# Feed-forward layers of a two-layer decoder in activations-stationary blocks, two of eight pairs of feature tiles by Strassen's seven products

## The chip, the core and the metric

The kernel runs on one core of one Trainium2 chip. The metric is the device time of one execution in microseconds (us). TensorE is called PE, VectorE DVE, ScalarE ACT, GpSimd POOL, SyncE SP.

## The reference

Two layers over 256 tokens of 2048 features, in float32. Each has a mixer (layer 0: mLSTM and Mamba-2 heads between w_in and w_out; layer 1: attention between w_qkv and w_o) and a feed-forward part, with a residual add behind each. The change concerns the feed-forward part, whose hidden width D_FF is 5632:

```
def swiglu(x, w_gate, w_up, w_down):
    return (jax.nn.silu(x @ w_gate) * (x @ w_up)) @ w_down
...
    for layer in range(DEPTH):
        xn = rms_norm(x, norm_mix[layer])
        ...
        x = x + swiglu(rms_norm(x, norm_ffn[layer]), *ffn_params[layer])
    return rms_norm(x, final_norm)
```

## The kernel before

The tokens are two tiles of 128 (`NT` = 2). A feature dimension is cut into k-tiles of 128 rows, an output dimension into strips of 512 columns (`STRIP`). Every float32 operand is split into a high part (a cast to fp32r on ACT) and a low part (the rest, a subtraction on DVE), and a product is hi·hi + hi·lo + lo·hi. Weights come as float32 by DMA on SP's queue into `raw` (two k-tiles of a strip, 512 KB), are cast to `wh` and subtracted to `wl` (`chunk`, L194 to L206, in high priority, so they stand early in the queues of ACT and DVE). There are 4 raw buffers and 3 of `wh` and `wl`. Activations stand transposed (features on partitions) in a `KT`, hi and lo side by side.

There are two ways to multiply. `lin_w` (L208) keeps 128x128 weight tiles stationary and streams the activations: per tile one matmul of 512 columns (`wh` with hi and lo, L219) and one of 256 (`wl` with hi, L221); results come out transposed. `lin_a` (L236) keeps activations stationary and streams the weights: per k-tile and token tile three matmuls of 512 columns (L249 to L251); results have tokens on partitions. The feed-forward part uses `lin_w` for gate and up (11 strips each), so `hT` needs no transposes, and `lin_a` for down (4 strips over 44 k-tiles), within `project_add`, which adds each strip to the residual `xres`, takes sums of squares (`sumsq`, ACT) and transposes the strip on PE for the next stage (`transpose_split`, four transposes into one bank `p_tr`, then casts and splits). `row_norm` (L179) turns the sums of squares into the norm's factor along rows: DVE `ss`, `rs`, POOL power `r`, DVE `dg`, and two matmuls `p_rb` on PE that broadcast it. The final norm's chain at the end is the same without `p_rb`.

Work of that kind is put off by `later` and given out by `tick`, once per pair of k-tiles, so that it stands between matmuls in PE's queue. Each engine runs its queue in order; the order is fixed when the program is built. PSUM has eight banks, six for accumulators (`acc_w`, `acc_a`) and two for everything else.

## Time and profile before

| | us |
|---|---|
| runs, median of 3 (lowest to highest) | 2657.42 (2655.51 to 2658.36) |
| the profiled execution | 2657.61 |
| its span in the trace | 2655.8 |
| PE busy | 2634.2 (99%) |
| DVE busy | 1621.2 (61%) |
| ACT busy | 1335.1 (50%) |

The span is the time from the first to the last instruction of the trace; the execution's own time has 1.8 us around it. Busy time is that of the instructions of an engine, and DVE and ACT work beside PE.

### The profile page before, as it was taken

To read this page: it belongs to the slowest core of one execution; us is meant where nothing else is said; L and a number is where in the kernel's file an instruction comes from. 1 tells how busy PE (TensorE), PEld (TensorE's weight loads), DVE (VectorE), ACT (ScalarE), POOL (GpSimd) and SP (SyncE) were. 2 spreads that over 40 slices of the span, in tenths; PEclk is the share of its full clock that TensorE was granted. 3 is DMA by queue.
4 is the path that set the end of the run, shared out by engine and by line. 5 is a ranking of instruction groups with operands and counts; after the bars stand their busy time and mean duration, and the time that the engine had idled before them with its cause. 6 is when DMAs were issued, how large, how long until landed. Compare 5 with 4: busy or idle time off the path is not lost.

```text
span 2655.8 us, 35559 instructions
## 1 busy us (share of the span) xinstructions
PE 2634.2 (99%) x13765; PEld 2246.7 (85%) x13765; DVE 1621.2 (61%) x2128; ACT 1335.1 (50%) x1906; POOL 45.8 (2%) x97
## 2 busy tenths in 40 slices
...
GB/s 231 168 191 182 184 182 204 167 187 219 189 190 182 185 188 185 188 184 189 190 191 190 190 182 169 177 171 163 185 183 190 190 190 190 190 190 206 193 195 160
DMA packets 254345, 496.86 MB, mean 187 GB/s; under 512 B 15656, under 2 KB 16048, under 8 KB 253792
## 3 DMA queue, kind: packets, MB, share of 16 engines
...
HBM read 492.39 MB, written 2.14 MB: 186 GB/s over the span
## 4 chain that ended last, share of the span: by engine, by line
PE 97%; DVE 1%; DMA 1%; issue 0%; ACT 0%; POOL 0%; SPq 0%; ACTq 0%; POOLq 0%; DVEq 0%
PE acc_w L219 35%; PE acc_w L221 18%; PE acc_a L249 13%; PE acc_a L251 13%; PE acc_a L250 13%; PE p_tr L169 1%; PE p_y L574 1%; DVE wl L205 1%; PE p_num L451 0%; DMA raw<-in_l_w_in 0%; PE p_qk L689 0%; PE p_o L719 0%; DMA xin<-in_x 0%; ACT wh L204 0%; PE p_pt L711 0%
## 5 line engine op out<-in xcount | busy, mean ns | idle before, releaser
L205 DVE TENSOR_TENSOR wl<-raw,wh 128x1024 fp32r<-128x1024 f32 (+1 forms) x913 | 1116.7, 1223 | 928.0 <-ACT wh L204 923.0
L204 ACT CAST wh<-raw 128x1024 fp32r<-128x1024 f32 (+1 forms) x913 | 958.9, 1050 | 1150.2 <-PE acc_w L219 551.0
L219 PE MATMUL acc_w<-x,wh 128*128 128x512 f32 x3328 | 1170.8, 397 | 0.0
L221 PE MATMUL acc_w<-x,wl 128*128 128x256 f32 x3328 | 929.1, 279 | 0.0
L219 PEld LDWEIGHTS acc_w<-x,wh 128*128 128x128 f32 x3328 | 624.8, 188 | 149.8
L221 PEld LDWEIGHTS acc_w<-x,wl 128*128 128x128 f32 x3328 | 626.9, 188 | 0.5
L219 PE MATMUL acc_w<-xa,wh 128*128 128x512 f32 x768 | 275.8, 403 | 1.1 <-DVE xa L118 1.1
L221 PE MATMUL acc_w<-xa,wl 128*128 128x256 f32 x768 | 215.9, 283 | 0.0
L219 PEld LDWEIGHTS acc_w<-xa,wh 128*128 128x128 f32 x768 | 145.0, 189 | 34.0 <-ACT wh L204 1.5
L249 PE MATMUL acc_a<-wh,xa 128*128 128x512 f32 x384 | 151.5, 395 | 0.0
L250 PE MATMUL acc_a<-wl,xa 128*128 128x512 f32 x384 | 150.8, 393 | 0.0
L251 PE MATMUL acc_a<-wh,xa 128*128 128x512 f32 x384 | 150.7, 393 | 0.0
L221 PEld LDWEIGHTS acc_w<-xa,wl 128*128 128x128 f32 x768 | 145.6, 190 | 1.0
L249 PE MATMUL acc_a<-wh,ha 128*128 128x512 f32 x352 | 137.5, 391 | 0.0
L251 PE MATMUL acc_a<-wh,ha 128*128 128x512 f32 x352 | 137.0, 389 | 0.0
L250 PE MATMUL acc_a<-wl,ha 128*128 128x512 f32 x352 | 137.0, 389 | 0.0
L249 PE MATMUL acc_a<-wh,hb 128*128 128x512 f32 x352 | 136.9, 389 | 0.0
L251 PE MATMUL acc_a<-wh,hb 128*128 128x512 f32 x352 | 136.9, 389 | 0.0
L250 PE MATMUL acc_a<-wl,hb 128*128 128x512 f32 x352 | 136.9, 389 | 0.0
L249 PE MATMUL acc_a<-wh,mx 128*128 128x512 f32 x256 | 100.4, 392 | 0.0
L251 PE MATMUL acc_a<-wh,mx 128*128 128x512 f32 x256 | 99.7, 390 | 0.0
L250 PE MATMUL acc_a<-wl,mx 128*128 128x512 f32 x256 | 99.6, 389 | 0.0
...
## 6 DMA issues: line engine op xcount, KB each, us to landing
raw<-in_l_w_in SPq DMA_DIRECT2D x191, 512.0 KB, 3.5
raw<-in_l_ffn_gate SPq DMA_DIRECT2D x176, 512.0 KB, 3.5
raw<-in_l_ffn_up SPq DMA_DIRECT2D x176, 512.0 KB, 3.5
raw<-in_l_ffn_down SPq DMA_DIRECT2D x176, 512.0 KB, 4.4
raw<-in_l_w_qkv SPq DMA_DIRECT2D x96, 512.0 KB, 3.6
raw<-in_l_w_out SPq DMA_DIRECT2D x64, 512.0 KB, 4.6
raw<-in_l_w_o SPq DMA_DIRECT2D x32, 512.0 KB, 3.5
rows<-scr POOLq DMA_DIRECT2D x10, 512.0 KB, 6.0
```

Of the source, the lines that this page charges most:

```text
L169: nc.tensor.transpose(pt[:, j * T + t * P:j * T + (t + 1) * P], src[t][:, c:c + P], ident)
L204: nc.scalar.copy(wh[:, ks, :], raw[:, ks, :])
L205: nc.vector.tensor_sub(wl[:, ks, :], raw[:, ks, :], wh[:, ks, :].bitcast(F32))
L219: nc.tensor.matmul(banks[f], wh[:, kk, fs], kt.both(k), start=k == 0, stop=False, skip_group_check=True)
L221: nc.tensor.matmul(banks[f][:, :T], wl[:, kk, fs], kt.parts(k)[0], start=False, stop=k == nk - 1, skip_group_check=True)
L249: nc.tensor.matmul(banks[t], xh[:, ts], wh[:, kk, :], start=k == 0, stop=False)
L250: nc.tensor.matmul(banks[t], xh[:, ts], wl[:, kk, :], start=False, stop=False)
L251: nc.tensor.matmul(banks[t], xl[:, ts], wh[:, kk, :], start=False, stop=k == nk - 1)
L574: nc.tensor.matmul(py[:, o0:o0 + SHD], e[:, lo:lo + P], y[st][:, hs], start=st == 0, stop=st == t, skip_group_check=True)
```

## The change

`lin_w` leaves the feed-forward part. `block` computes four quadrants at once with the activations stationary: two token tiles times a gate strip and an up strip (or two strips of down). Its step is a pair of k-tiles. A plain pair (P in `PLAN_X`, `PLAN_H`) is 8 products, a Strassen pair (S, the first and the third of each block, but none in the first hidden strip of a layer) 7, each of three matmuls of 512 columns. Products 2, 3, 4 go into the quadrants' banks F (banks 0 to 3), products 1, 7, 5, 6 into four banks E (4 to 7, `acc_e`); after the last S pair four additions of E (L389 to L393) give `pre`, which is added to F at the end of a hidden strip (L812), or at once to `xres` in down (L828). For an S pair DVE also makes four sums of weight tiles (L338 to L341), which take a raw buffer and get a `wh` and `wl` of their own, and, once per transposed half, four sums of activations (`activation_sums`). `held` keeps put-off work back until the E banks are read, since from the second hidden strip on `p_tr` uses the same banks 4 to 7. The hidden values have tokens on partitions now and are transposed on PE (two batches of four per strip). The hidden layer is done in groups of 4, 4 and 3 strips, each followed by the part of down that they feed: two blocks of 8, 8 or 6 pairs. x1 and x3 get their norm as a factor per token (`col_norm`), without `p_rb`; x2 keeps `row_norm`. Tile pools for weights are closed and opened again before each feed-forward stage and in the attention stage. The final gain is loaded strip by strip, the residual's input some 80 places earlier in SP's queue, and the gate weights of the mixer are split earlier at the start.

```diff
+PLAN_X, PLAN_H = "SPSPPPPP", "SPSPPPPP"
...
+    ring = {"acc": (0, 1, 2, 3, 4, 5), "aux": (6, 7)}
...
         clock[0] += 1
-        run_until(lambda p: p[0] > clock[0])
+        run_until(lambda p: held[0] or p[0] > clock[0])
...
+        ks = slice(2 * half, 2 * half + 2)
+        pair = pt.rearrange("p (a b) -> p a b", a=2)
+        summed = 2 * b + half in kt.sums
+        if summed:
+            xg = t2([P, 2, T], "xg")
+            if gcol is None:
+                nc.scalar.copy(xg, pair)
+            else:
+                for j in range(2):
+                    c = gcol + 4 * b + 2 * half + j
+                    nc.scalar.activation(xg[:, j, :], pair[:, j, :], AF.Copy, scale=pv[:, c:c + 1])
+            split(blk_[:, ks, 0, :], blk_[:, ks, 1, :], xg)
+            kt.sums[2 * b + half] = activation_sums(xg, gcol is not None)
+        elif gcol is None:
...
+        a11, a12, a21, a22 = a[:, 1, :P], a[:, 0, :P], a[:, 1, P:], a[:, 0, P:]
+        sf = t2([P, 4, P], "sf")
+        nc.vector.tensor_add(sf[:, 0, :], a21, a22)
+        nc.vector.tensor_sub(sf[:, 2, :], a11, a21)
+        nc.vector.tensor_sub(sf[:, 1, :], sf[:, 0, :], a11)
+        nc.vector.tensor_sub(sf[:, 3, :], a12, sf[:, 1, :])
+        pool, kind, n = (res, "skx", PLAN_X) if gains else (stage["stg"], "skh", PLAN_H)
+        sk = pool.tile([P, 4, 2, P], F32R, tag=kind, name=kind, bufs=n.count("S"))
+        split(sk[:, :, 0, :], sk[:, :, 1, :], sf)
...
+    def weights(src, row, summed):
+        pool = stage["stg"]
+        raw = pool.tile([P, 4, STRIP], F32, tag="raw", name="raw", bufs=4)
+        for i, (w, col) in enumerate(src):
+            nc.sync.dma_start(raw[:, 2 * i:2 * i + 2, :],
+                              w[row:row + 2 * P, col:col + STRIP].rearrange("(a p) f -> p a f", p=P))
+        def parts(of, cuts):
+            h = pool.tile([P, 4, STRIP], F32R, tag="wh", name="wh")
+            l = pool.tile([P, 4, STRIP], F32R, tag="wl", name="wl")
+            for c in cuts:
+                nc.scalar.copy(h[:, c, :], of[:, c, :])
+            for c in cuts:
+                nc.vector.tensor_sub(l[:, c, :], of[:, c, :], h[:, c, :].bitcast(F32))
+            return h, l
+        with tc.high_priority(offset=800):
+            if not summed:
+                return parts(raw, (slice(0, 2), slice(2, 4)))
+            sums = pool.tile([P, 4, STRIP], F32, tag="raw", name="sums", bufs=4)
+            nc.vector.tensor_sub(sums[:, 0:2, :], raw[:, 2:4, :], raw[:, 3:0:-2, :])
+            nc.vector.tensor_sub(sums[:, 2, :], raw[:, 2, :], sums[:, 1, :])
+            first = parts(raw, (slice(0, 3),))
+            nc.vector.tensor_sub(sums[:, 3, :], raw[:, 0, :], sums[:, 2, :])
+            return first + parts(sums, (slice(0, 2), slice(2, 4)))
+    def block(src, kt, row, nk, plan, after_sums=None, lead=1):
+        n = nk // 2
+        plan = plan[:n]
+        F = [None] * 4
+        pre = None
+        E = {}
+        def add(dst, a, b, start, stop):
+            (ah, al), (bh, bl) = a, b
+            nc.tensor.matmul(dst, ah, bh, start=start, stop=False)
+            nc.tensor.matmul(dst, ah, bl, start=False, stop=False)
+            nc.tensor.matmul(dst, al, bh, start=False, stop=stop)
+        last_s = plan.rfind("S")
+        held[0] = last_s >= 0
+        group = []
+        for j in range(n):
+            if plan[j] == "S":
+                wh, wl, sh, sl = weights(src, row + 2 * j * P, True)
+                tok = lambda k, t: tuple(x[:, t * P:(t + 1) * P] for x in kt.parts(k))
+                k2, k1 = 2 * j, 2 * j + 1
+                a11, a12, a22 = tok(k1, 0), tok(k2, 0), tok(k2, 1)
+                sk = kt.sums[j]
+                s1, s2, s3, s4 = [(sk[:, i, 0, :], sk[:, i, 1, :]) for i in range(4)]
+                b21, b11, b22 = [(wh[:, i, :], wl[:, i, :]) for i in range(3)]
+                t3, t1, t2_, t4 = [(sh[:, i, :], sl[:, i, :]) for i in range(4)]
+                prod = {1: (a11, b11), 2: (a12, b21), 3: (s4, b22), 4: (a22, t4),
+                        5: (s1, t1), 6: (s2, t2_), 7: (s3, t3)}
+                for p in (1, 7, 5, 6, 2, 3, 4) if j == 0 else (1, 2, 3, 7, 5, 6, 4):
+                    if p in (2, 3, 4):
+                        i = p - 2
+                        if F[i] is None:
+                            F[i] = bank(i, "acc_f")
+                        add(F[i], *prod[p], start=j == 0, stop=j == n - 1)
+                    else:
+                        if p not in E:
+                            E[p] = bank({1: 4, 7: 5, 5: 6, 6: 7}[p], "acc_e")
+                        add(E[p], *prod[p], start=j == 0, stop=j == last_s)
+                if j == last_s:
+                    pre = [t2([P, STRIP], "pre") for _ in range(4)]
+                    p1, v, u3, w = pre
+                    nc.scalar.copy(p1, E[1])
+                    nc.vector.tensor_add(v, p1, E[6])
+                    nc.vector.tensor_add(u3, v, E[7])
+                    nc.vector.tensor_add(v, v, E[5])
+                    nc.vector.tensor_add(w, u3, E[5])
+                    if after_sums is not None:
+                        after_sums(pre)
+                    held[0] = False
+            else:
+                group.append((j, weights(src, row + 2 * j * P, False)))
+                if len(group) < lead and j < n - 1 and n - j <= lead:
+                    continue
+                for i in range(4):
+                    t, s = divmod(i, 2)
+                    first = F[i] is None
+                    if first:
+                        F[i] = bank(i, "acc_f")
+                    for jj, (wh, wl) in group:
+                        for kk in range(2):
+                            xh, xl = kt.parts(2 * jj + kk)
+                            ts = slice(t * P, (t + 1) * P)
+                            add(F[i], (xh[:, ts], xl[:, ts]), (wh[:, 2 * s + kk, :], wl[:, 2 * s + kk, :]),
+                                start=first and jj == group[0][0] and kk == 0, stop=jj == n - 1 and kk == 1)
+                group = []
+            tick()
+        return F, pre
...
-        r, rb = row_norm(name, ss)
-        return nx, r, rb
-
-    def ffn(xt, rb, wg_, wu_, name):
-        hT = KT("h" + name, DFF // P)
-        rbh = cst.tile([P, T], F32, tag="rbh", name="rbh" + name)
-        nc.scalar.activation(rbh, rb, AF.Copy, scale=0.5)
-        for s in range(DFF // STRIP):
-            banks = lin_w(wg_, s * STRIP, xt, KD)
-            sgs = []
-            for b in range(2):
-                gs = t2([P, 2, T], "sg")
-                sgs.append(gs)
-                for j in range(2):
-                    lin_scaled(banks[2 * b + j], gs[:, j, :], rbh)
-                th = t2([P, 2, T], "thf")
-                nc.scalar.activation(th, gs, AF.Tanh)
-                nc.vector.scalar_tensor_tensor(gs, th, 1.0, gs, op0=OP.add, op1=OP.mult)
-                nc.vector.tensor_mul(gs, gs, rb[:, None, :].to_broadcast([P, 2, T]))
-            banks = lin_w(wu_, s * STRIP, xt, KD)
-            hb = hT.block(s)
-            for b in range(2):
-                ur = t2([P, 2, T], "ur")
-                for j in range(2):
-                    lin_sum(banks[2 * b + j], ur[:, j, :])
-                nc.vector.tensor_mul(ur, ur, sgs[b])
-                split(hb[:, 2 * b:2 * b + 2, 0, :], hb[:, 2 * b:2 * b + 2, 1, :], ur)
-        return hT
-
-    xt1, r1, rb1 = project_add(a["l0_w_out"], mixed, 32, "1", G_FFN0)
-    h0 = ffn(xt1, rb1, a["l0_ffn_gate"], a["l0_ffn_up"], "a")
-    xt2, r2, rb2_ = project_add(a["l0_ffn_down"], h0, DFF // P, "2", G_MIX1)
+        return nx, col_norm(name, ss)
...
+        def hidden(hT, i, s, plan):
+            F, pre = block(((wg_, s * STRIP), (wu_, s * STRIP)), xt, 0, KD, plan)
+            hs = []
+            for t in range(NT):
+                g, u = F[2 * t], F[2 * t + 1]
+                if pre is not None:
+                    for p, f in zip(pre[2 * t:2 * t + 2], (g, u)):
+                        nc.vector.tensor_add(p, p, f)
+                    g, u = pre[2 * t:2 * t + 2]
+                h = t2([P, STRIP], "h")
+                nc.scalar.activation(h, g, AF.Tanh, scale=rh[:, t:t + 1])
+                nc.vector.scalar_tensor_tensor(h, h, 1.0, g, op0=OP.add, op1=OP.mult)
+                nc.vector.scalar_tensor_tensor(h, u, rr[:, t:t + 1], h, op0=OP.mult, op1=OP.mult)
+                hs.append(h)
+            transpose_later(hT, i, hs, None, 1)
+        def down(hT, first, n, last):
+            for q in range(2):
+                c0 = 2 * q * STRIP
+                dst = [xr_[t][:, c0 + n_ * STRIP:c0 + (n_ + 1) * STRIP] for t in range(NT) for n_ in range(2)]
+                def add_all(what):
+                    for d, x in zip(dst, what):
+                        nc.vector.tensor_add(d, d, x)
+                if last and begin is not None:
+                    begin(2 * q)
+                    begin(2 * q + 1)
+                F, _ = block(((wd, c0), (wd, c0 + STRIP)), hT, first * STRIP, 4 * n, PLAN_H, add_all,
+                             lead=2 if last and q and name == "b" else 1)
+                add_all(F)
+                if last:
+                    for s in (2 * q, 2 * q + 1):
+                        finish(s)
+        ring["aux"] = (6, 7)
+        first = 0
+        for n in (4, 4, 3):
+            hT = KT(f"h{name}{first}", 4 * n)
+            hT.sums = {j: None for j in range(2 * n) if PLAN_H[j] == "S"}
+            for i in range(n):
+                hidden(hT, i, first + i, PLAN_X if first + i else "P" * len(PLAN_X))
+                ring["aux"] = (4, 5, 6, 7)
+            down(hT, first, n, first + n == DFF // STRIP)
...
```

**The order at the border into layer 0's feed-forward stage.** ACT there, in the kernel before; `sq` are the sums of squares of the last strip, `x_` the new activations, a number behind a name tells tiles of one name apart, and x2 at a row's end is a count:

```order
L257 ACTIVATE sq,ss_5686<-xres_5682 128x512 [waits DVE_49]
L257 ACTIVATE sq,ss_5686<-xres_5683 128x512 [waits DVE_49]
L204 CAST wh<-raw 128x1024 [waits DMAHW2_49,PE_49,Activation_49]
L191 COPY rb_6960<-p_rb 128x256 [waits PE_49]
L631 ACTIVATE rbha<-rb_6960 128x256 [waits Activation_49]
L117 ACTIVATE x_6990<-p_tr,pv 128x256 [waits PE_49]
```

The same place of the changed kernel; L147 is the cast of the transposed activations, L329 the weights' cast:

```order
L418 ACTIVATE sq,ss_5690<-xres_5686 128x512 [waits DVE_49]
L418 ACTIVATE sq,ss_5690<-xres_5687 128x512 [waits DVE_49]
L147 ACTIVATE x_7025<-p_tr,pv 128x256 [waits PE_49] x2
L147 ACTIVATE x_7025<-p_tr,pv 128x256 [waits DVE_49] x2
L329 CAST wh<-raw 128x1024 [waits DMAHW7_49]
L329 CAST wh<-raw 128x1024 [waits DMAHW0_49]
```

Before, weight casts stood between and ahead of these; now all four casts of x stand ahead of the stage's first weight cast. On PE, before:

```order
L251 MATMUL acc_a<-wh,mx_5779 128x512
L219 MATMUL acc_w<-x_6022,wh 128x512 [waits Activation_49]
L221 MATMUL acc_w<-x_6022,wl 128x256 [waits DVE_49]
L219 MATMUL acc_w<-x_6022,wh 128x512
L221 MATMUL acc_w<-x_6022,wl 128x256
...
L221 MATMUL acc_w<-x_6022,wl 128x256 [waits DVE_49]
L189 MATMUL p_rb<-dg,ones 128x128 [waits DVE_49,PE_49]
L189 MATMUL p_rb<-dg,ones 128x128 [waits DVE_49]
L169 MATMUL p_tr<-ident,xres_5682 128x128 [waits PE_49]
```

And of the changed kernel:

```order
L313 MATMUL acc_a<-wh,mx_5783 128x512
L202 MATMUL p_tr<-ident,xres_5686 128x128 [waits DVE_49]
L202 MATMUL p_tr<-ident,xres_5686 128x128 [waits PE_49]
L202 MATMUL p_tr<-ident,xres_5687 128x128 [waits DVE_49]
...
L202 MATMUL p_tr<-ident,xres_5687 128x128
L357 MATMUL acc_f<-wh,x_6026 128x512 [waits Activation_49]
L357 MATMUL acc_f<-wh,x_6026 128x512
L358 MATMUL acc_f<-wl,x_6026 128x512 [waits DVE_49]
L359 MATMUL acc_f<-wh,x_6026 128x512
```

The last strip's transposes have moved from behind eighteen weights-stationary matmuls to ahead of the stage's first matmul.

**The order in the first down block of a group of three strips.** DVE, in the kernel before, in the down stage of layer 0, where nothing but weights' subtractions and the adds of a strip stands:

```order
L205 TENSOR_TENSOR wl<-raw,wh 128x1024 [waits DMAHW4_49,Activation_49]
L621 TENSOR_TENSOR xres_5682<-xres_5682,acc_a 128x512 [waits PE_49]
L621 TENSOR_TENSOR xres_5683<-xres_5683,acc_a 128x512 [waits PE_49]
L205 TENSOR_TENSOR wl<-raw,wh 128x1024 [waits DMAHW5_49,Activation_49]
L205 TENSOR_TENSOR wl<-raw,wh 128x1024 [waits DMAHW6_49,DVE_49,Activation_49]
L118 SCALAR_TENSOR_TENSOR x_12264<-p_tr,pv,x_12264 128x256 [waits Activation_49] x2
```

DVE of the changed kernel, layer 0, from the subtraction for the next block's first S pair on; L391 to L393 are the additions of E banks, L145 the low part of the transposed hidden strip (its two halves):

```order
L331 TENSOR_TENSOR wl<-raw,wh 128x1536 [waits Activation_49]
L392 TENSOR_TENSOR pre<-pre,acc_e 128x512 [waits DVE_49]
L393 TENSOR_TENSOR pre<-pre,acc_e 128x512
L828 TENSOR_TENSOR xres_5686<-xres_5686,pre 128x512 [waits DVE_49]
L828 TENSOR_TENSOR xres_5687<-xres_5687,pre 128x512
L828 TENSOR_TENSOR xres_5687<-xres_5687,pre 128x512 [waits DVE_49]
L338 TENSOR_TENSOR sums<-raw 128x1024 [waits DMAHW7_49,DMAHW0_49]
L145 TENSOR_TENSOR ha_11849<-p_tr,ha_11849 128x2x256 [waits Activation_49]
L339 TENSOR_TENSOR sums<-raw,sums 128x512 [waits DVE_49]
L145 TENSOR_TENSOR ha_11849<-p_tr,ha_11849 128x2x256
```

And PE of the changed kernel at the same place; `acc_f<-wh,ha_11517` is the end of a plain pair, `acc_e` the next block's first product, `ha_11849` the last hidden strip:

```order
L359 MATMUL acc_f<-wh,ha_11517 128x512
L202 MATMUL p_tr<-ident,h 128x128 [waits DVE_49]
L202 MATMUL p_tr<-ident,h 128x128 x3
L357 MATMUL acc_e<-wh,ha_11189 128x512 [waits Activation_49]
L358 MATMUL acc_e<-wl,ha_11189 128x512 [waits DVE_49]
L359 MATMUL acc_e<-wh,ha_11189 128x512
L202 MATMUL p_tr<-ident,h 128x128 [waits DVE_49]
L202 MATMUL p_tr<-ident,h 128x128 x3
L357 MATMUL acc_f<-wh,ha_11849 128x512 [waits Activation_49]
L358 MATMUL acc_f<-wl,ha_11849 128x512
...
L359 MATMUL acc_f<-wh,ha_11849 128x512 [waits DVE_49]
```

The transposes of the last hidden strip and the split of its low part, which the following plain pair reads (L359, low part times `wh`), stand behind the additions of E banks, and these behind a weight subtraction.

## Rows read from the trace of the kernel before

**Rows 1.** The page: busy time of the engines; the chain that ended last.
```profile
PE 2634.2 (99%) x13765; PEld 2246.7 (85%) x13765; DVE 1621.2 (61%) x2128; ACT 1335.1 (50%) x1906; POOL 45.8 (2%) x97
...
PE 97%; DVE 1%; DMA 1%; issue 0%; ACT 0%; POOL 0%; SPq 0%; ACTq 0%; POOLq 0%; DVEq 0%
```

**Rows 2.** Windows by stage: us, busy per engine (instructions), clock, DMA share, GB/s.
```profile
787.20:1287.10 499.90, 499.04 (x2829) 432.68 (x2828) 317.61 (x400) 239.53 (x315) 0.69 (x1) 1.00 0.59 186
1287.10:1529.40 242.30, 242.30 (x1083) 200.58 (x1082) 120.28 (x114) 102.92 (x115) 0.00 (x0) 1.00 0.57 191
1529.40:1816.00 286.60, 285.81 (x1540) 245.85 (x1539) 180.75 (x258) 162.94 (x270) 0.69 (x1) 1.00 0.58 175
...
1916.00:2407.00 491.00, 490.21 (x2831) 428.40 (x2831) 316.62 (x401) 239.62 (x315) 0.69 (x1) 1.00 0.60 189
2407.00:2646.60 239.60, 239.60 (x1058) 198.07 (x1056) 118.47 (x112) 97.40 (x105) 0.55 (x1) 1.00 0.55 187
2646.60:2655.80 9.20, 0.01 (x1) 0.00 (x0) 2.48 (x6) 2.45 (x5) 0.55 (x1) 0.73 0.68 228
```

**Rows 3.** Timeline of PE, stage of w_out: start, us, what.
```profile
700.97 0.60 PE L169 MATMUL p_tr<-ident,xres 128*128 128x128 f32 x4
...
701.64 0.40 PE L250 MATMUL acc_a<-wl,mx 128*128 128x512 f32 x1
```

**Rows 4.** DVE by form: busy us, mean ns, idle before and releaser.
```profile
L205 DVE TENSOR_TENSOR wl<-raw,wh 128x1024 fp32r<-128x1024 f32 x911 | 1115.3, 1224 | 928.0 <-ACT wh L204 923.0
...
L642 DVE SCALAR_TENSOR_TENSOR sg<-thf,sg 128x512 f32<-128x512 f32 x44 | 30.1, 684 | 0.0
...
L115 DVE TENSOR_TENSOR wgl<-wg,wgh 128x1536 fp32r<-128x1536 f32 x1 | 1.8, 1759 | 0.2 <-ACT wgh L114 0.2
```

**Rows 5.** ACT by form, the same columns.
```profile
L204 ACT CAST wh<-raw 128x1024 fp32r<-128x1024 f32 x911 | 957.7, 1051 | 1150.2 <-PE acc_w L219 551.0 <-PE acc_a L251 459.4 <-issue 87.1
...
L114 ACT CAST wgh<-wg 128x1536 fp32r<-128x1536 f32 x1 | 1.5, 1478 | 0.0
```

**Rows 6.** The page, DMA issues: KB each, median us to landing.
```profile
raw<-in_l_ffn_gate SPq DMA_DIRECT2D x176, 512.0 KB, 3.5
```

**Rows 7.** Timeline of DVE in gate and up of layer 0.
```profile
810.58 1.23 DVE L205 TENSOR_TENSOR wl<-raw,wh 128x1024 fp32r<-128x1024 f32 x1 [1.60 <-ACT wh L204]
811.72 0.42 DVE L228 TENSOR_TENSOR ls<-acc_w,ls 128x256 f32<-128x256 f32 x1
```

**Rows 8.** Timeline of PE at the border into layer 0's feed-forward stage.
```profile
790.27 0.28 PE L221 MATMUL acc_w<-x,wl 128*128 128x256 f32 x1
791.41 0.68 PE L189 MATMUL p_rb<-dg,ones 128*128 128x128 f32 x4 [0.86 <-DVE dg L188]
```

**Rows 9.** Timeline of ACT at that border.
```profile
788.38 0.62 ACT L257 ACTIVATE sq<-xres 128x512 f32<-128x512 f32 x1
788.90 0.18 ACT L257 ACTIVATION_READ_ACCUMULATOR sq<-xres 128x1 f32 x1
...
792.86 0.46 ACT L117 ACTIVATE x<-p_tr,pv 128x256 fp32r<-128x256 f32 x1
793.87 0.47 ACT L117 ACTIVATE x<-p_tr,pv 128x256 fp32r<-128x256 f32 x1 [0.55 <-DVE x L118]
```

**Rows 10.** Timeline of DVE at that border.
```profile
786.93 1.28 DVE L621 TENSOR_TENSOR xres<-xres,acc_a 128x512 f32<-128x512 f32 x2
...
789.74 0.16 DVE L182 TENSOR_REDUCE ss<-ss 128x2 f32<-128x8 f32 x1
790.00 0.17 DVE L109 TENSOR_SCALAR rs<-ss 128x2 f32<-128x2 f32 x1
790.98 0.48 DVE L188 TENSOR_SCALAR dg<-ident,r 128x128 f32<-128x128 f32 x2 [0.80 <-POOL r L110]
```

**Rows 11.** Timeline of the tail.
```profile
2646.65 0.69 DVE L746 TENSOR_TENSOR xres<-xres,acc_a 128x512 f32<-128x512 f32 x1
...
2649.15 0.55 POOL L110 TENSOR_TENSOR rf<-rs,mhalf 128x1 f32<-128x1 f32 x1 [3.53 <-DVE rs L109]
```

More of the change, by code (lines that the diff above doesn't have):

```diff
@@ L194, in chunk @@
     def chunk(w, k, col, step=KC):
-        raw = stg.tile([P, KC, STRIP], F32, tag="raw", name="raw", bufs=4)
-        wh = stg.tile([P, KC, STRIP], F32R, tag="wh", name="wh")
-        wl = stg.tile([P, KC, STRIP], F32R, tag="wl", name="wl")
+        raw = stage["stg"].tile([P, KC, STRIP], F32, tag="raw", name="raw", bufs=4)
+        wh = stage["stg"].tile([P, KC, STRIP], F32R, tag="wh", name="wh")
+        wl = stage["stg"].tile([P, KC, STRIP], F32R, tag="wl", name="wl")
         for i in range(0, KC, step):
@@ new lines, in block @@
+    def block(src, kt, row, nk, plan, after_sums=None, lead=1):
[45 more added lines that the diff above has]
+                    held[0] = False
+            else:
+                group.append((j, weights(src, row + 2 * j * P, False)))
[15 more added lines that the diff above has]
+        return F, pre
@@ L606, in hybrid_trunk, with col_norm @@
         strips[st[0]](int(st[1]))
-    xr_ = [blk([P, D], f"xres{t}") for t in range(NT)]
+    xr_ = [long([P, D], f"xres{t}") for t in range(NT)]
     for t in range(NT):
         nc.sync.dma_start(xr_[t], x_in[t * P:(t + 1) * P, :])
+    def col_norm(name, ss4):
+        ss = sml.tile([P, NT], F32, tag="ss", name="ss" + name)
+        nc.vector.tensor_reduce(ss, ss4, axis=AX.X, op=OP.add)
+        r = cst.tile([P, NT], F32, name="r" + name)
+        rsqrt_mean(r, ss, D)
+        return r
     def project_add(w, kt, nk, name, gcol):
-        nx = KT("x" + name, KD)
+        nx = KT("x" + name, KD, long)
+        nx.sums = {j: None for j in range(KD // 2) if PLAN_X[j] == "S"}
         ss = cst.tile([P, NT, 4], F32, name="ss" + name)
+        turn["acc"] = 4
         for s in range(4):
```

101 lines of the change are left out of this document (73 added, 28 removed).

## The prediction

> **What bounds the kernel now.** I read the page's busy line and its chain first [rows 1]: PE is busy for 2634.2 of 2655.8 us and carries 97% of the chain, while DVE stands at 61% and ACT at 50%. So time is columns streamed through PE, and whatever takes columns away is worth their price until DVE or ACT can't follow. The table by stage came next [rows 2]: the granted clock is 1.00 in every stage but the last 9.2 us, and the four feed-forward windows are 499.9 (gate and up of layer 0), 242.3 (down of layer 0), 491.0 and 239.6 us, together 1472.8. In them PE never waits for more than a moment, so their prices per matmul can be taken by division.
>
> The last down window has 1056 matmuls of 512 columns and nothing else but two records: 239.6/1056 = 0.2269 us each, which I take for every activations-stationary matmul. Gate and up of a layer are 1408 pairs of a 512- and a 256-column matmul: 0.3550 us a pair in layer 0 and 0.3487 in layer 1, for the same instructions. A batch of four transposes costs little [rows 3]: from its start at 700.97 to that of the second matmul behind it, 701.64, are 0.67 us, where without it one pitch of 0.227 would stand, so a batch is 0.445. Layer 0's down window holds six of these: 242.3 − 6 × 0.445 = 239.6 again.
>
> By 512/0.2269 the stream does not run at the rate of one column per 2.4 GHz cycle, which would be 0.2133. The Trainium skill ("TensorE: Matmul & The Clock Gate", Wait — 56ns, not 53.3ns?) gives 215.7 ns from start to start for 512 columns; by that 6144 matmuls would take 1325 us, 69 less than below. The trace has 226.9 over 239.6 us at a clock of 1.00, so I use the trace.
>
> **What the change does to PE.** A plain pair of k-tiles on four quadrants is 8 products of 3 matmuls, 24; a Strassen pair is 7, so 21. A hidden strip has 8 pairs, two of them Strassen: 186 matmuls, and 192 in the first strip. A layer is 192 + 10 × 186 = 2052, and its down blocks are 4 × 186 + 2 × 138 = 1020. Both layers: 6144, or 1394.1 us. The hidden strips must now be transposed, 44 batches, 19.6 us. Ten batches of x transposes that lie in these windows or at their borders stay, 4.4. Sum 1418.1, against 1472.8: **−54.7 us**. Without Strassen there would be 6336 matmuls, 1437.6 + 24.0 = 1461.6, so the layout alone is worth 11.2 and the 192 missing matmuls 43.6. Bounds: 0.2269 is a stage of the same form, and nothing but the stationary tile changes.
>
> **What DVE gets.** A plain pair is two subtractions of 1024, 2 × 1.224 [rows 4]. A Strassen pair is a sum of 1024, two of 512 at 0.685, a subtraction of 1536 at 1.759 and two of 1024: 6.80. A hidden strip: 6 × 2.448 + 2 × 6.80 + 12 operations of 512 (four sums of E banks, four adds of F, four for h) 8.22 + two splits 1.37 + about 1.1 of activation sums = 38.9 us. PE's strip is 186 × 0.2269 + 0.89 = 43.1. DVE is at 90%, where it was at 64% [rows 2]. It fits, but queue order decides. ACT has per strip 12 casts of 1.05 for plain pairs, for each Strassen pair one of 1536 at 1.478 and two of 1.05 [rows 5], four tanh and copies at some 0.62 and four casts of h and its sums: some 25 us. DMA: a plain pair asks 1 MB in 5.45 us, a Strassen pair in 4.77, 220 GB/s for a moment; 228 were moved at a share of 0.68 [rows 2], and a load of 0.5 MB lands in 3.5 us [rows 6]. I cost it at nothing; the cover is the four raw buffers, and the sums take one of them.
>
> I walked the strip from the end of its last plain pair: pair 7 to 5.46, S0 to 10.24, P1 15.70, S2 20.48, P3 25.94. The E banks end just before 20.48, are added on DVE between weight subtractions, and are wanted by transposes at the pair behind P3's start and end. I find the add v done at 22.2 where PE asks at 22.5, and w at 26.4 where it asks at 27.3: no stall, with 0.3 us to spare. These use the overlap of independent DVE operations: L228 begins 1.14 after a subtraction of 1.23 began [rows 7]. For the small misses I take 0.1 us in each of about 30 blocks: **+3** (bounds 0 and 0.75 × 32 = 24, the rival below).
>
> The Trainium skill ("VectorE: DVE Perf Modes", Terms) says the next operation can't issue until the pipe is empty, and its Rules for kernel authors ask for few operations; this change adds 312, by the count of DVE's instructions in program order. The trace shows 0.09 us of overlap [rows 7]. Without overlap v would be done at 22.5 or later, about 0.5 a block, and the time about 2650.
>
> **Where the queues make PE wait.**
> - *Borders into the feed-forward stages (two).* Before, weight casts stood ahead and PE worked for 3 us after the last acc_a; then it waited 0.86 for p_rb [rows 8]. In the new order ACT's next weight cast stands behind two sq and four x casts, and PE's first acc_f behind eight transposes, in a stage whose pools are new. From the last matmul: add 0.85, transposes 0.9, x casts behind them to 4.2 (two casts are 1.0 apart, at 792.86 and 793.87, the second behind a DVE split [rows 9]), weight cast 1.05 to 5.3, subtraction 1.22 to 6.5. PE works 1.4 of that: 5.0 each, **+10**. Bounds 2 × 2 (if the four x casts run dense behind the transposes and a load is there) and 2 × 8 (if loads of the new pools also start only here: 3.5 more).
> - *Border into attention.* row_norm stays here, and its p_rb now stands ahead of the first acc_w: the last add 0.7, sq 0.8 [rows 9], ss and rs 0.4, pow 0.8, dg 0.5 [rows 10]. That is 3.1 of idle where 0.79 stood (286.60 less 285.81 in [rows 2]): **+2.3** (bounds 0 and 4).
> - *The 3-strip groups' first down block (one a layer).* On DVE the subtraction of 1536 for the next block's S0 stands ahead of the adds u3 and w. It needs a weight buffer that P3 releases at 25.94: cast 1.48 to 27.5, subtraction to 29.5, u3 and w to 31.0, three xres adds to 33.0, a sum of 1024 to 34.2, and only then the lo part of the h that P4's lo·hi matmuls need, to 34.9. PE has from 25.94 two transposes, three acc_e and eight hi matmuls, 3.4 us: idle 5.6, twice, **+11.2**. Bounds 0 and 2 × 7.5 (no work hoisted).
> - *The second such block of layer 0*, where x2's transposes and adds crowd, **+1.5** (0 to 3). *Tail:* the end goes add, sq, reduce, pow, scale as before [rows 11], but both token tiles' last quadrants end together, so four adds and two sq lie in the chain: **+1.2** (0 to 3). *Start:* gains are split earlier by ACT and DVE, xres is loaded 80 places earlier on SP: **+1** (0 to 2).
>
> Sum: 3 + 10 + 2.3 + 11.2 + 1.5 + 1.2 + 1 = 30.2. The profiled execution took 2657.61, the median of the runs is 2657.42, no difference. 2657.6 − 54.7 + 30.2 = 2633.1, **2633 us**.
>
> **Rivals.**
> - *Hidden losses* (0.17): borders at 2 each, the down block's hoisted work longer than I find, and the rest covered. Then 2657.6 − 54.7 + 4 to 9: 2607 to 2612. For it: PE waited some 13 us in all before. Against it: the waits I list are in one engine's order, which no scheduler changes on the chip.
> - *DVE late at the E banks* (0.18, the other side): transposes and the next S0 use banks 4 to 7, so each us by which the adds v, u3, w end late is a us of PE in each of 32 blocks with Strassen (20 hidden strips, 12 down blocks). With 24.5 us of gain left, the no-change point is 0.77 us late; at 1.5 it is 2681. For it: 90% of DVE, and 0.3 of slack. Against it: in before DVE's waits were for ACT's casts, 923 us [rows 4], so weights can run ahead.
> - *Pace of the untouched weights-stationary strips* (0.05): the same 1408 pairs took 499.9 and 491.0 us with tiles in other places, 0.0063 a pair; 1280 such pairs remain and all their tiles move, ±8 us, to 2641.
>
> **How the numbers follow.** Forecast 0.60, with a range of its own of 2620 to 2648: the bounds of the border and down-block terms, not all at one end. No change means within 0.2%, 2652.1 to 2662.7, about what a measurement of this kernel can tell. Faster: 0.60 + 0.17 + 0.03 of the third = 0.80. Same: 0.07 of the second and 0.02 of the third. Slower: 0.11 of the second. For 8 in 10 I go down to 2608, which leaves out a third of the first rival (0.06), and up to 2660, which leaves out 0.13.
>
> **What would show it.** Layer windows of about 720 us for 3072 matmuls and waits; block matmuls at 0.227; DVE near 90% in hidden strips; PE idle of 5 us at the two borders ended by ACT's weight cast, and of 5 to 6 in each 3-strip group ended by a DVE split. Wrong would be: idle in every strip at p_tr or acc_e with DVE as the releaser (second rival); gaps with DMA as the releaser; a pace per matmul off 0.227 by more than 0.002, which is 12 us.

## The result, and the profile after

The changed kernel takes 2644.12 us (median of 4 runs, 2640.99 to 2644.46), the kernel before 2656.8 (2655.51 to 2658.36) in the runs beside it: a ratio of 0.9949, with a 95% interval of 0.9932 to 0.9967. Faster, as forecast, but by 12.7 us where 24 were forecast. The profiled execution is the shortest of the four, 2640.99 us, with a span of 2639.2; the other three have spans of 2642.2 to 2642.6.

The page, busy time and chain, against [rows 1]:

```profile
PE 2596.3 (98%) x12333; PEld 2166.5 (82%) x12333; DVE 1937.3 (73%) x2440; ACT 1375.2 (52%) x1854; POOL 47.0 (2%) x97
...
PE 94%; DVE 2%; issue 1%; ACT 1%; DMA 1%; POOL 0%; ACTq 0%; POOLq 0%; DVEq 0%
```

The windows by stage, cut where the last matmul of a stage ends, against [rows 2]: mixer of layer 0, feed-forward part, attention, feed-forward part, tail. The columns are the window, its length, busy time of PE, PEld, DVE, ACT and POOL, the granted clock, the DMA share and GB/s.

```profile
0.00:793.40 793.40, 779.36 (x3969) 659.21 (x3970) 508.64 (x774) 436.58 (x694) 43.81 (x92) 1.00 0.62 188
793.40:1516.30 722.90, 715.66 (x3185) 589.48 (x3184) 591.54 (x656) 358.55 (x395) 0.69 (x1) 0.99 0.58 194
1516.30:1907.40 391.10, 388.28 (x2014) 330.89 (x2013) 241.37 (x345) 220.64 (x372) 0.69 (x1) 1.00 0.56 170
1907.40:2628.50 721.10, 712.88 (x3169) 586.93 (x3167) 592.15 (x655) 356.03 (x390) 0.69 (x1) 1.00 0.57 193
2628.50:2639.20 10.70, 0.17 (x1) 0.00 (x0) 3.59 (x11) 3.36 (x6) 1.10 (x2) 0.65 0.54 196
```

Cut in the same way (2646.45 for the end of the last matmul), the kernel before has 787.2, 742.2, 387.1, 729.9 and 9.4. So the two feed-forward parts gained 28.1 us, 1472.1 to 1444.0, and the rest lost 11.5: 6.2 in the mixer, whose code is hardly touched, 4.0 in attention, 1.3 in the tail. Less than two thirds of what the feed-forward parts gained is left: 16.6 us of span between the two profiles.

What PE waited for in the whole span (total, times, longest):

```profile
PE acc_f L357 <- ACT wh L329: 6.2, 2, 3.2
...
PE acc_w L281 <- DVE xa L148: 3.8, 2, 2.7
...
PE acc_f L359 <- DVE hb L145: 2.7, 1, 2.7
PE p_tr L202 <- DVE x L148: 2.3, 1, 2.3
PE acc_e L358 <- DVE wl L331: 1.6, 1, 1.6
PE p_y L735 <- DVE dec L719: 1.5, 1, 1.5
PE p_tr L202 <- DVE pre L391: 1.4, 1, 1.4
```

The borders (6.2), the two 3-strip groups (`hb`, `wl`, `pre` of layer 0 or 1), the border into attention (`x` L148) are there as forecast; the longer of the two waits for `xa` and the one for `dec` are in the mixer. No row is a wait that comes back in every strip.

The clock, in windows of 1 us behind the border into layer 1's feed-forward part (PE's busy time second, the granted clock third from the end):

```profile
1910.00:1911.00 1.00, 0.00 (x0) 0.00 (x0) 0.78 (x4) 0.60 (x2) 0.19 (x1) 1.00 0.90 297
1911.00:1912.00 1.00, 0.00 (x0) 0.00 (x0) 0.73 (x2) 1.00 (x2) 0.00 (x0) 0.74 1.00 375
1912.00:1913.00 1.00, 0.73 (x2) 0.50 (x2) 0.75 (x1) 1.00 (x2) 0.00 (x0) 0.50 1.04 399
...
1917.00:1918.00 1.00, 1.00 (x4) 0.72 (x4) 1.00 (x1) 0.84 (x1) 0.00 (x0) 0.50 1.06 410
1918.00:1919.00 1.00, 1.00 (x5) 0.86 (x4) 0.94 (x2) 0.21 (x1) 0.00 (x0) 0.85 1.05 406
1919.00:1920.00 1.00, 1.00 (x6) 0.78 (x6) 0.47 (x1) 0.00 (x0) 0.00 (x0) 1.00 1.06 412
```

PE idled for two of these windows, and the clock then stands at 0.50, 1.2 GHz in place of 2.4, until 1918: 4 matmuls touch the window from 1917 and 6 that from 1919. The prediction has no term for this. One less the clock, summed over such windows, is 3.4 us here, 1.7 behind layer 0's border, 3.4 behind the waits of layer 0's 3-strip group, 1.7 at the border into attention and 1.7 behind the wait at 26 us: 11.9. PE is idle for 2.6 us of these stretches, where the lower clock costs nothing, so 11.9 is an upper bound.

### The profile page after: what moved, and what is told of

It is laid out like the page before. It is cut to its first block, busy times and chain, and to the rows that moved or that the text cites. A ratio compares the mean times of both kernels' runs of the same rounds, so it can differ in the third digit from the quotient of the medians.

```text
span 2639.2 us, 32482 instructions
## 1 busy us (share of the span) xinstructions
PE 2596.3 (98%) x12333; PEld 2166.5 (82%) x12333; DVE 1937.3 (73%) x2440; ACT 1375.2 (52%) x1854; POOL 47.0 (2%) x97
## 4 chain that ended last, share of the span: by engine, by line
PE 94%; DVE 2%; issue 1%; ACT 1%; DMA 1%; POOL 0%; ACTq 0%; POOLq 0%; DVEq 0%
PE acc_f L358 15%; PE acc_f L359 15%; PE acc_f L357 15%; PE acc_w L281 10%; PE acc_a L311 7%; PE acc_a L312 7%; PE acc_a L313 7%; PE acc_w L283 5%; PE acc_e L358 2%; PE acc_e L359 2%; PE acc_e L357 2%; PE p_tr L202 1%; PE p_y L735 1%; DVE wl L267 0%; DVE wl L331 0%
## 5 line engine op out<-in xcount | busy, mean ns | idle before, releaser
L329 ACT CAST wh<-raw 128x1024 fp32r<-128x1024 f32 (+1 forms) x464 | 495.2, 1110 | 459.5 <-PE acc_f L359 424.2
L331 DVE TENSOR_TENSOR wl<-raw,wh 128x1024 fp32r<-128x1024 f32 (+1 forms) x464 | 582.9, 1295 | 202.4 <-ACT wh L329 201.0
L267 DVE TENSOR_TENSOR wl<-raw,wh 128x1024 fp32r<-128x1024 f32 (+1 forms) x385 | 470.0, 1221 | 338.9 <-ACT wh L266 337.7
L357 PE MATMUL acc_f<-wh,x 128*128 128x512 f32 x1168 | 458.0, 392 | 6.2 <-ACT wh L329 6.2
L358 PE MATMUL acc_f<-wl,x 128*128 128x512 f32 x1168 | 457.1, 391 | 0.3 <-DVE wl L331 0.3
L359 PE MATMUL acc_f<-wh,x 128*128 128x512 f32 x1168 | 456.5, 391 | 0.0
L357 PEld LDWEIGHTS acc_f<-wh,x 128*128 128x128 f32 x1168 | 220.1, 189 | 51.9 <-ACT wh L329 6.7
L358 PEld LDWEIGHTS acc_f<-wl,x 128*128 128x128 f32 x1168 | 220.4, 189 | 46.7 <-DVE wl L331 1.7
L359 PEld LDWEIGHTS acc_f<-wh,x 128*128 128x128 f32 x1168 | 220.2, 188 | 45.2
L329 ACT CAST wh<-sums 128x1024 fp32r<-128x1024 f32 x128 | 128.0, 1048 | 133.5 <-PE acc_f L359 129.4
L281 PE MATMUL acc_w<-x,wh 128*128 128x512 f32 x512 | 185.0, 405 | 0.0
L331 DVE TENSOR_TENSOR wl<-sums,wh 128x1024 fp32r<-128x1024 f32 x128 | 150.9, 1220 | 18.8 <-ACT wh L329 18.8
L283 PE MATMUL acc_w<-x,wl 128*128 128x256 f32 x512 | 143.2, 281 | 0.0
L281 PEld LDWEIGHTS acc_w<-x,wh 128*128 128x128 f32 x512 | 96.7, 189 | 22.3
```

The lines of the kernel that those rows point to most:

```text
L267: nc.vector.tensor_sub(wl[:, ks, :], raw[:, ks, :], wh[:, ks, :].bitcast(F32))
L281: nc.tensor.matmul(banks[f], wh[:, kk, fs], kt.both(k), start=k == 0, stop=False, skip_group_check=True)
L283: nc.tensor.matmul(banks[f][:, :T], wl[:, kk, fs], kt.parts(k)[0], start=False, stop=k == nk - 1, skip_group_check=True)
L329: nc.scalar.copy(h[:, c, :], of[:, c, :])
L331: nc.vector.tensor_sub(l[:, c, :], of[:, c, :], h[:, c, :].bitcast(F32))
L357: nc.tensor.matmul(dst, ah, bh, start=start, stop=False)
```

## The experiments

Twelve kernels were run in three batches: all_plain, filler, casts_first and group3; gates_late, three_hidden, all_mended and att_mended; the last four. Each batch ran on another chip, with the kernel before beside it. That took 2657.55, 2666.04 and 2665.68 us (all its runs lie between 2647.0 and 2668.0), so times are best compared within a batch, and stages by their profiles. This table has the stages of each profile in us, cut as above (the start of a stage's last matmul plus 0.227):

| kernel | time | mixer | ffn 0 | attention | ffn 1 | tail |
|---|---|---|---|---|---|---|
| all_plain | 2673.76 | 795.9 | 737.8 | 390.0 | 736.9 | 10.8 |
| filler | 2642.04 | 796.0 | 722.1 | 391.3 | 720.6 | 10.8 |
| casts_first | 2643.34 | 799.2 | 722.8 | 391.2 | 721.2 | 10.7 |
| group3 | 2632.95 | 794.3 | 717.2 | 390.3 | 715.4 | 10.6 |
| gates_late | 2641.95 | 790.6 | 723.4 | 390.3 | 721.8 | 10.7 |
| three_hidden | 2618.84 | 795.8 | 711.5 | 390.2 | 708.6 | 10.7 |
| all_mended | 2620.26 | 791.6 | 712.4 | 390.4 | 711.6 | 10.6 |
| att_mended | 2618.29 | 790.2 | 712.4 | 389.8 | 712.3 | 10.7 |
| change_again | 2644.02 | 793.9 | 722.9 | 391.1 | 721.2 | 10.6 |
| sums_late | 2647.13 | 797.0 | 726.2 | 391.5 | 721.0 | 10.7 |
| three_mended | 2606.17 | 792.9 | 706.9 | 390.0 | 705.0 | 10.7 |
| four_mended | 2737.92 | 796.4 | 769.4 | 392.6 | 769.1 | 10.7 |

**all_plain: the layout without Strassen.**

```diff
-PLAN_X, PLAN_H = "SPSPPPPP", "SPSPPPPP"
+PLAN_X, PLAN_H = "PPPPPPPP", "PPPPPPPP"
```

> All pairs plain, the layout of the change without Strassen: 192 matmuls more. If a Strassen product saved is worth its full pitch on PE and DVE's sums cost nothing but the waits in the two 3-strip groups (7.6 us idle and 3.4 us of lowered clock in the profile of the change): 2644 + 43.6 - 11 = about 2677 us, DVE busy falling by some 250 us. If Strassen's sums cost PE time all over (DVE late at the E banks): well under 2677, 2655 or less.

2673.76 us, 0.66% more than before (ratio 1.0066, 1.0041 to 1.0092). The feed-forward parts take 1474.7, 30.7 more than in the change: 43.6 for 192 matmuls, less 11.1 of waits and clock in the 3-strip groups, which are gone, would be 32.5. So Strassen's products are worth their pitch to within 2 us of 43.6, and the layout alone gains nothing: 2.6 us more than the 1472.1 of before, and what it was to save, 11.2 by the prediction, is about what the waits (7.7) and the clock (5.1) at the borders cost in the change.

**filler: is it the idle time that lowers the clock?** In the first hidden strip of each layer, ahead of its pairs:

```diff
+            need((kt.name, 3))
+            jb = bank(3, "junk")
+            for i in range(12):
+                nc.tensor.matmul(jb, kt.block(3)[:, 0, 0, :P], kt.both(0), start=True, stop=True)
```

> Twelve matmuls of 512 columns without use stand on PE behind the last transposes at both borders into the feed-forward stages, where PE waits for ACT's weight casts; they read the first new x block, so they run while PE would be idle. If the granted clock falls to 0.50 because PE idles there: the low stretches behind 798 us and 1911 us vanish, 1.7 and 3.4 us less, the waits for the casts stay, about 2639 us. If the clock falls for another reason (the start of the weights' transfers, the casts themselves): no change, 2644, or up to 3 us more for the filler.

2642.04 us, 2 less than the change, which is within the spread of either kernel's runs. The clock in every 1 us window from 790 to 812 and from 1905 to 1925 is 1.00 (this kernel's borders are at 796.0 and 1909.3), so work without use in PE's idle time kept it up: idling is the cause. Two of these microseconds, 3.7 to 5.7 behind the border, where the change stands at 0.74 and 0.50:

```profile
1913.00:1915.00 2.00, 1.91 (x8) 1.07 (x7) 1.47 (x3) 2.00 (x3) 0.00 (x0) 1.00 1.02 389
```

But it gave less than the clock's sum: the 73rd matmul behind the border (the first behind three pairs) came 22.22 and 22.14 us after it where the change has 23.39 and 24.38, so 1.2 and 2.2 of 1.7 and 3.4. And in layer 1 most of it went again, at the 3-strip group. The change, and below it filler:

```profile
2586.00:2588.00 2.00, 0.00 (x0) 0.00 (x0) 2.00 (x4) 0.58 (x1) 0.00 (x0) 1.00 0.00 0
...
2590.00:2592.00 2.00, 2.00 (x10) 1.65 (x9) 0.41 (x1) 0.00 (x0) 0.00 (x0) 1.00 0.00 0
```

```profile
2588.00:2590.00 2.00, 1.57 (x6) 1.25 (x7) 2.00 (x4) 0.00 (x0) 0.00 (x0) 0.85 0.00 0
2590.00:2592.00 2.00, 2.00 (x6) 1.59 (x5) 0.18 (x1) 0.00 (x0) 0.00 (x0) 0.50 0.00 0
```

In the change PE is idle for 2 us and the clock is at 1.00 behind it; in filler, with the same waits (2.7 us for `hb` among them), the windows from 2588 have 0.85, 0.50 and 0.80. A wait of this length lowers the clock in one execution and not in another. The changed kernel itself shows it in its two profiles, at the wait of 26 us, 2.70 long in the first profile and 2.74 in change_again. The first's windows, and below them change_again's:

```profile
30.00:32.00 2.00, 2.00 (x12) 1.91 (x11) 0.06 (x1) 1.14 (x2) 0.00 (x0) 0.68 0.93 325
32.00:34.00 2.00, 2.00 (x8) 1.81 (x8) 1.95 (x3) 1.18 (x4) 0.00 (x0) 0.50 0.17 64
```

```profile
30.00:32.00 2.00, 2.00 (x16) 1.87 (x15) 0.00 (x0) 0.93 (x1) 0.00 (x0) 1.00 0.97 339
32.00:34.00 2.00, 2.00 (x13) 1.74 (x13) 1.86 (x3) 1.06 (x4) 0.00 (x0) 1.00 0.24 91
```

By one less the clock change_again loses the same 11.9 in all: nothing here, and 1.7 in layer 1's 3-strip group in its place.

**casts_first: weight casts ahead of the casts of x at the borders.** The last strip's transposes read a copy of `ident` that is made with the first weight tile of the new stage:

```diff
+                if j == 0 and kt.home is long and last_s < 0:
+                    nc.vector.scalar_tensor_tensor(ident_b, group[0][1][0][:, 0, :P].bitcast(F32), 0.0, ident,
+                                                   op0=OP.mult, op1=OP.add)
+                    idt["now"] = ident_b
```

> At both borders the last strip's transposes are made to depend on the first weight cast of the new stage, so casts of weights stand ahead of the casts of x on ACT and pair 0's matmuls ahead of p_tr on PE. Theory (ACT's order sets the border): PE's first acc_f comes 2.4 us earlier at each border, and less of the clock is lost: 2634 to 2639 us. Rival (the new pools' loads set it, since the third load waits for the last matmul of the old stage): PE waits later instead, at pairs 1 and 2, and the time stays at 2644.

2643.34 us: nothing that can be told from the change. PE's first matmul did come 2.4 and 2.3 us earlier (2.62 after the border, 4.98 in the change; 2.63, 4.89), but PE still idled for 2.5 and 1.1 us there, the clock fell to 0.50 as before (in the three windows of 1 us from 805 on), and the 73rd matmul came at 23.07 and 22.88, 0.3 and 1.5 earlier. PE's idle time there fell only from 4.0 and 3.7 us to 3.6 and 3.5, and one less the clock from 1.7 and 3.4 to 1.7 and 1.7: half a repair of the order left most of both standing.

**group3: the E banks read earlier in the 3-strip groups.**

```diff
-                F, _ = block(((wd, c0), (wd, c0 + STRIP)), hT, first * STRIP, 4 * n, PLAN_H, add_all,
+                F, _ = block(((wd, c0), (wd, c0 + STRIP)), hT, first * STRIP, 4 * n,
+                             "SPPPPP" if n == 3 and q == 0 else PLAN_H, add_all,
```

> The first down block of a 3-strip group has one Strassen pair (the first) in place of two, so the E banks are read one plain and one Strassen pair earlier; 3 matmuls more in each layer, 1.4 us. Theory: the waits there (3.0 us and 3.4 of clock in layer 0, 4.6 in layer 1) vanish: about 2635 us. Rival: the lo part of the last hidden strip is late for another reason, the waits stay: 2645.

2632.95 us, 9 to 10 less than filler and casts_first beside it and 11 less than the change. Six matmuls more, and both feed-forward parts 5.7 shorter: the waits there are gone with the clock's loss. In layer 1, 1.7 of the 5.7 comes from elsewhere: behind that border, which the edit leaves alone, the clock stood at 0.50 for 3.4 us in this profile and for 6.8 in the change's. The window that holds layer 0's last two down blocks has PE busy throughout:

```profile
1440.00:1511.40 71.40, 71.40 (x328) 58.81 (x327) 59.61 (x73) 37.06 (x51) 0.00 (x0) 1.00 0.48 160
```

**gates_late: the mixer's gate weights split late again.**

```diff
+    nc.vector.tensor_scalar(wg[:, 0, 31:32], qT[:, 4, 0:1], 0.0, None, op0=OP.mult)
     split(wgh, wgl, wg)
```

> The change, with the split of the mixer's gate weights made to wait for a result of the second strip of w_in, as late as it was before the change. Theory: the 2.7 us wait of PE at 26 us for a split of xa, and the 1.7 us of lowered clock behind it, come from this split standing early on ACT and DVE; without it the stage before the feed-forward part is 3 to 4 us shorter, about 2640.5. Rival: what stands late there is the x transposes for another reason; the wait stays, 2644.

2641.95 us. In the change PE waits here:

```profile
26.24 0.28 PE L283 MATMUL acc_w<-xa,wl 128*128 128x256 f32 x1
29.21 0.50 PE L281 MATMUL acc_w<-xa,wh 128*128 128x512 f32 x1 [2.70 <-DVE xa L148]
```

With the split late that wait is gone, and the mixer takes 790.6 where the change has 793.4 and 793.9 in its two profiles. The eight profiles with the early split have 793.4 to 799.2, the four with the late one and nine temporary buffers 790.2 to 792.9 (four_mended, with seven, 796.4). So the mixer gained 2.8 to 3.3 us, where the theory had 3 to 4; the median is 2 below the change's, which was not run beside it. The other 3.4 over the 787.2 of before stay: PE waits 2.0 for `dec` here, a wait that before doesn't have. It wasn't followed further.

**three_hidden: one Strassen pair more, on top of group3.**

```diff
-PLAN_X, PLAN_H = "SPSPPPPP", "SPSPPPPP"
+PLAN_X, PLAN_H = "SPSPSPPP", "SPSPPPPP"
```

> As group3, and three Strassen pairs in place of two in each of the 20 hidden strips that have them: 60 matmuls less, 13.6 us. By full durations DVE would need 43.3 us in a strip where PE needs 42.4; by the overlap in the trace (DVE 84% busy in the hidden strips of the change) 40.5. Theory (DVE still hidden): about 2619.5. Rival (the other side of the prediction: DVE late at the E banks): half or more of the gain goes in each strip, 2627 to 2640, with PE idle at p_tr or acc_e, released by DVE, in every strip.

2618.84 us. Its feed-forward parts are 711.5 and 708.6, 12.5 less than group3's, of 13.6 for the 60 matmuls, though the clock behind layer 0's border cost 1.7 more here than in group3's profile. PE shows no wait for DVE that comes back in every strip. DVE late at the E banks was the rival on the other side; at a heavier load than the change's (DVE busy for 36.8 to 40.6 us of a strip of 42.5) it still did not come.

**all_mended and att_mended: nothing ahead of the first weight cast.** all_mended has group3, gates_late, the dependence of casts_first, and the same for the last strip's sums of squares; att_mended does that at the border into attention too:

```diff
+        def norm(mark):
+            nc.vector.tensor_scalar(ss[:, :, 3], mark, 0.0, None, op0=OP.mult)
+            for t in range(NT):
+                sumsq(ss[:, t, 3:4], xr_[t][:, 3 * STRIP:])
+            return col_norm(name, ss)
```

> group3 and gates_late together, and at both feed-forward borders the last strip's sums of squares too wait for the first weight cast, so nothing stands ahead of it on ACT. Theory: PE's first matmul comes within 1.5 us of the last one of the old stage, no lowered clock behind it: 2633 - 3.5 - 8 = about 2621. Rival (the loads of the new pools set the border, as casts_first suggests: it gained 1 us): 2628.

> As all_mended, and at the border into attention the last transposes and sums of squares wait for the first weight cast of w_qkv. Theory: the 2.3 us wait and about 1.7 us of clock there vanish, 4 less than all_mended, about 2617. Rival: p_rb or the late sums of squares make PE wait later in the first attention strip: same as all_mended.

all_mended took 2620.26 us: its feed-forward parts are 4.8 and 3.8 us shorter than group3's. PE's timeline at layer 0's border, which in the change has 4.98 us from the end of acc_a to the first acc_f:

```profile
791.39 0.39 PE L323 MATMUL acc_a<-wh,mx 128*128 128x512 f32 x1
791.62 0.61 PE L367 MATMUL acc_f<-wh,x 128*128 128x512 f32 x2
793.70 0.50 PE L368 MATMUL acc_f<-wl,x 128*128 128x512 f32 x1 [1.46 <-DVE wl L341]
```

Its clock is 1.00 in all windows from 790 to 798. So the rival, that the new pools' loads set the border, fell: ACT's order set it. At the border into attention the same did less: 2618.29 us, 2 less than all_mended where 4 were expected, and by the profiles the attention stage is only 0.6 shorter. There the lowered clock is gone, but the wait moved, as the rival had it, in part to `p_rb`:

```profile
1502.65 0.61 PE L292 MATMUL acc_w<-x,wh 128*128 128x512 f32 x2
1504.72 0.39 PE L294 MATMUL acc_w<-x,wl 128*128 128x256 f32 x1 [1.46 <-DVE wl L277]
...
1510.20 0.68 PE L261 MATMUL p_rb<-dg,ones 128*128 128x128 f32 x4 [1.48 <-DVE dg L260]
```

**change_again, sums_late, three_mended, four_mended.** The changed kernel for comparison, and three kernels beside it:

```diff
                     nc.vector.tensor_add(v, p1, E[6])
+                    nc.vector.tensor_add(v, p1, E[6])
```

> The changed kernel once more, beside the kernels of this call: 2641 to 2646 us, feed-forward stages of 722 to 724 us each in its profile, the stage before them 793 to 799.

> The change with the first addition of the E banks done twice, so v, u3 and w are 0.69 us later in each of 32 blocks, with the same results. By the prediction's walk (0.3 us to spare): 0.4 us of PE in each block, 12 us more than the change, about 2656, with PE idle at p_tr released by DVE in most strips. If there is more slack than the walk found: within 2 us of the change, 2642 to 2646.

change_again took 2644.02 us, 0.1 off the first measurement (0.9932 of before beside it, 0.9909 to 0.9955). sums_late took 2647.13, 3.1 more and not 12. In its profile layer 0's part is 3.3 longer (726.2, 722.9), at the 3-strip group, layer 1's is the same, and the mixer, which the edit leaves alone, 3.1 longer; the other strips do not wait. DVE's timeline in a hidden strip:

```profile
953.52 0.68 DVE L391 TENSOR_TENSOR pre<-pre,acc_e 128x512 f32<-128x512 f32 x1
954.24 0.69 DVE L392 TENSOR_TENSOR pre<-pre,acc_e 128x512 f32<-128x512 f32 x1
```

And PE's there:

```profile
954.00 0.39 PE L359 MATMUL acc_f<-wh,x 128*128 128x512 f32 x1
954.26 0.65 PE L202 MATMUL p_tr<-ident,h 128*128 128x128 f32 x4
```

v is done at 954.20, and p_tr begins at 954.26 without a wait: the program, built again with the longer chain, has put p_tr further back among the matmuls: 24 stand between it and the last acc_e here, 12 in the change, where v is done at 947.13 and p_tr begins at 947.31. The spare time of a walk holds for one order, and the order gives way.

> att_mended with three Strassen pairs in the hidden strips. If the 60 matmuls are worth their pitch here as in three_hidden: 2618.3 - 13.6 = about 2605. If DVE has no room left once PE no longer waits at the borders: 2612 or more.

> att_mended with four Strassen pairs in the hidden strips (every other pair), and seven in place of nine temporary buffers, since memory asks for it. DVE would need 36.2 + 2 x 4.35 = 44.9 us in a strip where PE needs 41.7. If DVE becomes the bound: 20 strips x 2.5 us more than three_mended, about 2655. If overlap still hides it: 13.6 less than three_mended, 2591.

three_mended is att_mended with three Strassen pairs, and the best kernel here: 2606.17 us, 0.979 of before (0.9767 to 0.9813) and 37.9 us less than change_again beside it. four_mended (`"SPSPSPSP"`, and 7 temporary buffers for 9) lost 132 us to it. DVE's busy share is no higher in windows from 900 to 1100 us, 177.41 of 200 in place of 177.88; what came is the mechanism of the prediction's second rival, waits at p_tr and acc_e for the last E addition, and at acc_e for the splits that read p_tr's banks:

```profile
PE p_tr L212 <- DVE pre L404: 20.6, 7, 3.7
PE acc_e L368 <- DVE pre L404: 15.1, 8, 2.9
PE acc_e L368 <- DVE hb L145: 9.7, 4, 2.4
PE acc_e L368 <- DVE ha L145: 7.9, 4, 2.7
```

With the fourth Strassen pair the E banks are read only at the last pair but one, and the next strip's first pair and the transposes want them right behind. The waits bring the clock down too: it stands at 0.50 in 18 stretches, 78.5 us in all, where three_mended has one of 3.4, so up to 37.5 of the 132 us (one less the clock) go that way. How much of the loss is the fourth pair and how much the missing buffers was not told apart.

## Why the prediction was right, and where it was off

**The gain on PE** (−54.7) and the steady strip were right. From the first acc_e of one hidden strip to that of the next block are 43.09 to 43.27 us in the trace (42.16 behind a down block, where no transposes stand in the strip), the sum was 43.1, and PE doesn't wait in them. Two of layer 0's strips:

```profile
844.00:887.12 43.12, 43.12 (x196) 35.68 (x195) 35.02 (x41) 22.21 (x24) 0.00 (x0) 1.00 0.58 195
930.30:973.39 43.09, 43.09 (x196) 35.69 (x194) 35.28 (x39) 21.67 (x23) 0.00 (x0) 1.00 0.57 195
```

DVE is busy for 35 to 37 us in these and the strip between them, 83%, where 38.9 and 90% were forecast. all_plain shows the 192 matmuls at their price, to within 2 us.

**The sum of the feed-forward parts** was right in total, 1443.8 (1418.1 + 25.7) against 1444.0, but not in its make-up. The waits there sum to some 15 us where 25.7 stood, so that the totals agree to 0.2 us is luck. At the borders the mechanism and its order were as walked (the cast of weights at 798.38, forecast 5.3 us after the last matmul, measured 4.98; the subtraction 6.23, forecast 6.5):

```profile
793.17 0.39 PE L313 MATMUL acc_a<-wh,mx 128*128 128x512 f32 x1
...
798.38 0.95 PE L357 MATMUL acc_f<-wh,x 128*128 128x512 f32 x2 [3.15 <-ACT wh L329]
799.63 0.80 PE L358 MATMUL acc_f<-wl,x 128*128 128x512 f32 x1 [0.31 <-DVE wl L331]
```

That is 4.0 and 3.7 us of idle, not 5.0 each. In the 3-strip groups it was 3.2 in layer 0 and 4.5 in layer 1 where 5.6 stood twice. In layer 1 it was released by u3's addition and by the low part of h, as named, in layer 0 by the split of the next block's weights (1.6 by DVE's subtraction, 0.7 by the cast) and by the cast of h (0.7). The +3 for small misses and +1.5 for layer 0's second block have no row. What filled most of the gap of 10 is what the sum did not have: up to 8.5 us by the lowered clock behind three of these four places.

**The step that failed** is the list of losses: it priced each wait by its length and had no term for the clock behind it. That is up to 11.9 us over the profile by one less the clock; filler gave back 3.4 of the 5.1 at the borders. The kernel before never showed it, since behind its first 11 us PE's longest wait was 0.86 us [rows 8] and the clock only left 1.00 in the tail [rows 2]; I read that as a property of the kernel and not as one of its short waits. The Trainium skill ("TensorE: Matmul & The Clock Gate", What's actually happening) has the rule, that the lower clock is the default and activity lifts it, at moments not tied to the kernel's start. The traces agree: 0.50 and 1.00 are its levels, work without use kept it at 1.00, and the same wait of the changed kernel lowered it in one execution and not in another.

**Start** was mis-sized: +1 was forecast, the mixer lost 6.2. I priced the early split of the gate weights by the time that ACT and DVE spend on it, not by the splits of xa that stand behind it and that PE waits for: 2.7 us, and 1.7 of clock in this profile (change_again has neither that loss nor a shorter mixer, so not all of the 6.2 is accounted for). 1.5 more are the wait for `dec`. **Attention** was +2.3 (its five terms make 3.2 and not 3.1) and came to 4.0; a wait of 2.3 is there, with 1.7 of clock. The **tail** was 1.3 for 1.2. These three make 7 of the 11 us between forecast and median; 3 are the profiled execution being that much shorter than the median.

**The rivals.** Hidden losses: no, the borders cost 4 each and their clock. DVE late at the E banks: not in the change, nor with three Strassen pairs; sums_late shows that its price, a us for a us in each block, doesn't hold when the order is planned with the longer chain, and four_mended shows the mechanism where the plan leaves it no room. The rule of the Trainium skill ("VectorE: DVE Perf Modes", Terms), which gave 2650, is nearer to the result than my 2633, but not by its reason: the hidden strips kept 43.1 to 43.3 us and no wait for DVE comes back in them. Pace of the untouched strips: no, PE is busy for 779.4 us of the mixer where it was 777.7, and the lowered clock covers the 1.7 between.
